# Weight sums made by DMA: an earlier start in the input projection, and all four sums for the last up block

## The chip, the cores and the metric

The kernel runs on one core of a Trainium2 chip. A core has TensorE (PE, matmuls), VectorE (DVE), ScalarE (ACT), GpSimd (POOL) and SyncE (SP), each with a program of its own that it works through in order, and 16 DMA engines that all of them can give transfers to. The metric is the device time of one execution in microseconds (us). The kernel before takes 2088.9 us, the median of three runs (2087.66 to 2093.45).

## The reference, cut to what matters

The block has 512 positions of 2048 channels in float32. An input projection of 4096 columns feeds two token mixers; their normalised outputs go through one output projection; then comes a feed-forward part with 12288 up columns:

```python
h = _rmsnorm(x, norm1_g[l])
p = jnp.einsum('bsd,de->bse', h, w_in[l])
...
y = jnp.concatenate([_rmsnorm(y_gm, gm_out_g[l]), _rmsnorm(y_lru, lru_out_g[l])], axis=-1)
x = x + jnp.einsum('bse,ed->bsd', y, w_out[l])
h = _rmsnorm(x, norm2_g[l])
up = jnp.einsum('bsd,df->bsf', h, ffn_w_up[l])
up = _causal_dwconv(up, ffn_conv_w[l], ffn_conv_b[l])
gate, val = jnp.split(up, 2, axis=-1)
x = x + jnp.einsum('bsf,fd->bsd', jax.nn.gelu(gate) * val, ffn_w_down[l])
```

## The kernel before, in words

**Products in three passes.** Every float32 operand is split into a rounded part h and a rest l (`split`: ACT writes h on L125, DVE writes l = value - h on L126), and each product is three matmuls, h·h, h·l and l·h.

**The projections.** `project` (L171) does one block of 512 columns of the input projection: four chunks `kc` of weights, 1 MB each, loaded by SP into `wraw` (two buffers) and split in two halves of 1024 elements a partition into `wh`/`wl` (three buffers each). It is called eight times; the first call also loads and splits the activations, and is the one with `with_row`. What hangs between the chunks (gates, scans of the recurrent mixer) is passed in as `between`. `out_proj` (L518) does the output projection in the same way, two chunks a call, eight calls: first the four calls of half 1, then the four of half 0. In these stages a scheduler orders the instructions of each engine, except where `manual_schedule` keeps an engine in the order in which the code is written.

**The feed-forward part** works with 2x2 blocks and seven products instead of eight (a Strassen-like scheme). A unit is one block of 256x512 weights; `up_block` (L883) takes 8 units, one for each 256 channels, and has 24 calls in 12 pairs (gate columns, then value columns): units 0 to 191. `down_block` takes the gated rows by chunks of 8, 8 and 6 units for each of four column groups: units 192 to 279. A unit is 7 products of 2 x 3 matmuls (L855), 42 in all. Its seven weight operands are three of the four quarters and four sums of quarters. They are brought by a stream of elements (`Weights`, and `Acts` for the row operands) through three steps: `load` puts the quarters in a slot `q` (three slots; four in the down blocks), `sums` forms the sums on DVE (L609 a pair, then L612 and L613 one each; for `Acts` L636 to L638), `pair` splits all seven (L125 on ACT, L126 on DVE, 1792 elements a partition). `prepare` writes these steps so that the sums of an element stand ahead of the pair of the element before it, on DVE in that order, and a load stands behind the pair that frees its slot.

**Made units.** For some units the sums are not formed on DVE but in memory: POOL issues DMAs that copy a row list of `w_m` into a DRAM tile `made` and then add others to it (`accum_op`), six DMAs for a unit whose four sums are made ("whole"), two for a unit with two sums made ("halved"). SP then loads the made tile (512 KB, or 256 KB for a halved one) and three quarters (384 KB) in place of four quarters (512 KB). A whole unit has no sums on DVE, a halved one keeps L612 and L613. Before the change units 0 to 7, 192 to 199, 216 to 231 and 248 to 261 are whole, and 184 to 191, the last up block, are halved: 46 x 6 + 8 x 2 = 292 DMAs. The 48 of units 0 to 7 stand behind the x loads of the output projection's first half on POOL; the other 244 are handed out by `make` after each unit of the up blocks, evenly over units 0 to 183.

**Who shares POOL's queue.** POOL also issues the loads of gate weights (`graw`, L346), of `vgb`, `ws`, `bsb` and x, and in the up blocks the stores of gated rows (`ad`, L924), four in a row of some 20 us for each pair of blocks, which wait for DVE. In program order the made DMAs of a pair of blocks stand between and behind these four, so they go out in a burst behind the fourth.

**The end of an up block.** `combine` (L868) adds the seven PSUM tiles: ACT copies the first (`c`, L871), DVE does seven additions (L872 to L879), which give the tiles back to PE for the next block. There are 8 such tiles, and a block uses 7. In the order of ACT the copy stands behind the splits that the last unit's `prepare` has written.

Of the kernel before, what the change touches and what calls it, by code (L numbers as in the profile page):

```python
# [8 lines left out]
F32 = mybir.dt.float32  # L9
# [3 lines left out]
ALU = mybir.AluOpType  # L13

P = 128
# [49 lines left out]


def made_units():

    n_up = 24 * 8
    starts = [n_up + 4 * (c[0] - CHUNKS[0][0]) for c in CHUNKS]  # L70
    whole = list(range(8))
    for c, s in zip(CHUNKS, starts):
        whole += range(max(s - 8, n_up), s + len(c))
    return whole, list(range(n_up - 8, n_up))
# [3 lines left out]
def hybrid_block(ctx: ExitStack, tc: tile.TileContext, x, xT, w_in, w_out, w_up, w_dn, w_m4, w_m2, w_dl, wab, wsT, vec, bs, vgb, fg, out):  # L78
# [92 lines left out]
    def project(w, block, act, channel_major, between=None, with_row=None):  # L171
# [7 lines left out]
        for kc in range(4):  # L179
# [12 lines left out]
            if between is not None:  # L192
                between(kc)
        return ps
# [92 lines left out]
    with tc.manual_schedule(engines={E.SP, E.Activation, E.DVE}):  # L287
        px0 = project(w_in, B_X, xg, True, norm1, load_rows)

# [228 lines left out]
    def out_proj(d, half, ysrc, rstd, x_in, between=None):  # L518
        ps = [bank() for _ in range(NS)]
        for c in range(2):  # L520
# [6 lines left out]
            if between is not None:  # L527
                between(c)
        for st in range(NS):
# [26 lines left out]

    in_order = ExitStack()
    in_order.enter_context(tc.manual_schedule(engines={E.Pool}))
# [33 lines left out]
    class Weights:  # L592
# [5 lines left out]
        def load(self):  # L598
# [3 lines left out]
            else:  # L602
                nc.sync.dma_start(q[:, 4 - self.made.shape[1]:4], self.made)
                nc.sync.dma_start(q[:, 4:7], self.src[:, 0:3])

        def sums(self):
            q = self.q
            if self.made is None:
                nc.vector.tensor_tensor(q[:, 2:4], q[:, 5:7], q[:, 7:8].broadcast_to([P, 2, 256]), ALU.add)  # L609
            elif self.made.shape[1] == 4:  # L610
                return
            nc.vector.tensor_tensor(q[:, 1], q[:, 2], q[:, 6], ALU.add)  # L612
# [78 lines left out]
    made = {}  # L691
# [4 lines left out]

    whole, halved = made_units()
    rows = {}  # L700
    for k, u in enumerate(whole):
        t = tc.dram_tile([P, 4, 256], F32, name=f"made{u}")
        flat = t.rearrange("(a b) c d -> a (b c d)", b=2)
        first, second = (w_m4[k, i:i + 512].rearrange("(a b) c -> a (b c)", b=8) for i in (0, 512))
        made[u], rows[u] = t, [[(flat[h], src[h]) for h in (slice(0, 32), slice(32, 64))] for src in (first, second)] + [
            [(t[:, 0:2], w_m4[k, 1024:1280].rearrange("(p a) c -> p a c", p=P))],
            [(t[:, 0], w_m4[k, 1280:1408])],
        ]
    for k, u in enumerate(halved):
        t = tc.dram_tile([P, 2, 256], F32, name=f"made{u}")  # L710
        view = t.rearrange("(a b) c d -> a (b c d)", b=4)
        made[u], rows[u] = t, [[(view, w_m2[k, i * 256:i * 256 + 256].rearrange("(a b) c -> a (b c)", b=8))] for i in range(2)]
# [10 lines left out]
    def make(todo, n):  # L723

        for _ in range(min(n, len(todo))):
            r, dst, src = todo.pop(0)
            how = {"accum_op": ALU.add} if r else {}
            nc.gpsimd.dma_start(dst, src, max_dma_last_dim=8192, **how)  # L728
# [91 lines left out]
    pools["ps"] = psum("q0", 7)  # L820
# [304 lines left out]
```

## Time and profile before

| what | value |
|---|---|
| median of the runs | 2088.9 us |
| the profiled execution: time, and its span | 2092.59 us, 2090.9 us |
| mean granted TensorE clock | 0.995 |
| PE busy | 2045.2 us, 98% |
| DVE busy | 1738.6 us, 83% |
| POOL busy | 283.2 us, of it made DMAs 209.9 us (292 x 863 ns) |
| DMA: software queue (POOL's), hardware queue (SP's) | 24.3%, 34.4% of 16 engines' span |

The table is of one profiled execution. PE is busy nearly all the time, so a gain has to come out of the few stretches in which it stands still or runs at the lower clock; the rows further down show where these are. A busy PE is not PE at its peak, since matmuls overlap: in a stretch the count of matmuls tells more than the busy time.

### The profile page before, as it was taken

The page shows a single profiled execution, that of the slowest core. Times are in us where ns is not written, and L with a number is a line of the kernel's source. Part 1 is how long each engine was busy: PE and PEld are TensorE (multiplying, and loading weights), DVE is VectorE, ACT ScalarE, POOL GpSimd, SP SyncE. Part 2 cuts the span into 40 slices and gives each one's busy share as a digit, 9 for nine tenths or more (in the row PEclk, how much of TensorE's full clock was granted, in tenths as well). Part 3 has the DMA queues.
Part 4 walks back from the last instruction along what each step waited for, and adds up shares of the span by engine and source line. Part 5 has one row for each costly group of instructions (what it writes and reads, how often), then busy time and mean ns, then how long its engine had stood idle before and what let it go on. Part 6 is the DMA issues. An engine that isn't in the chain of part 4 may idle for free.

```text
span 2090.9 us, 34973 instructions
## 1 busy us (share of the span) xinstructions
PE 2045.2 (98%) x14528; PEld 1923.7 (92%) x14528; DVE 1738.6 (83%) x2199; ACT 906.7 (43%) x887; POOL 283.2 (14%) x434
## 2 busy tenths in 40 slices
PE   9999999999989999999999999999998999999998
PEld 7888888888789999999999999999998999999996
DVE  7598982735379999999998999999999989979986
ACT  6445322423264444444444444444455345445343
POOL 1000000033010312212213122122110000000001
PEclk9999999999999999999999999999999999999999
DMA  8222322479263857657658577576566568658564
GB/s 286 92 81 87 115 101 89 157 218 290 85 182 104 212 158 183 179 158 202 177 153 212 141 188 184 155 199 182 151 188 214 191 200 285 190 188 277 182 227 160
DMA packets 102832, 366.93 MB, mean 175 GB/s; under 512 B 14096, under 2 KB 20624, under 8 KB 89232
## 3 DMA queue, kind: packets, MB, share of 16 engines
q1 hardware_dynamic: 65808, 244.20, 34.4%
q0 software_dynamic: 36288, 119.83, 24.3%
q8 instruction: 113, 1.85, 0.4%
q10 hardware_dynamic: 576, 0.66, 0.1%
q14 instruction: 47, 0.39, 0.1%
HBM read 332.13 MB, written 103.02 MB: 208 GB/s over the span
## 4 chain that ended last, share of the span: by engine, by line
PE 71%; DVE 20%; DMA 5%; issue 2%; ACT 1%; SPq 0%; DVEq 0%; ACTq 0%
PE qs L855 42%; PE ps L161 9%; PE ps L163 9%; PE ps L162 9%; DVE wl L126 8%; DMA q<-w_up 4%; DVE q L609 2%; DVE al L126 1%; DVE q L612 1%; DMA q<-ad 1%; DVE cv L919 1%; DVE gate L919 1%; PE qs L162 1%; PE qs L161 1%; PE qs L163 1%
## 5 line engine op out<-in xcount | busy, mean ns | idle before, releaser
L855 PE MATMUL qs<-ah,wh 128*128 128x256 f32 x2688 | 765.3, 285 | 12.3 <-DVE pad L872 8.6
L855 PE MATMUL qs<-ah,wl 128*128 128x256 f32 x2688 | 762.1, 284 | 2.8 <-DVE wl L126 2.8
L855 PE MATMUL qs<-al,wh 128*128 128x256 f32 x2688 | 761.8, 283 | 2.1 <-DVE al L126 2.1
L125 ACT CAST wh<-q 128x1792 fp32r<-128x1792 f32 (+1 forms) x282 | 476.8, 1691 | 593.1 <-PE qs L855 340.8
L126 DVE TENSOR_TENSOR wl<-q,wh 128x1792 fp32r<-128x1792 f32 (+1 forms) x282 | 567.7, 2013 | 47.8 <-ACT wh L125 47.6
L855 PEld LDWEIGHTS qs<-ah,wh 128*128 128x128 f32 x2688 | 517.0, 192 | 16.7 <-DVE pad L872 10.5
L855 PEld LDWEIGHTS qs<-ah,wl 128*128 128x128 f32 x2688 | 516.9, 192 | 3.6 <-DVE wl L126 3.6
L855 PEld LDWEIGHTS qs<-al,wh 128*128 128x128 f32 x2688 | 517.0, 192 | 2.3 <-DVE al L126 2.3
L855 PE MATMUL qs<-wh,ah 128*128 128x256 f32 x1232 | 350.5, 285 | 8.5 <-ACT c L871 4.0
L855 PE MATMUL qs<-wl,ah 128*128 128x256 f32 x1232 | 350.0, 284 | 0.8 <-DVE wl L126 0.6
L855 PE MATMUL qs<-wh,al 128*128 128x256 f32 x1232 | 349.7, 284 | 0.0
L855 PEld LDWEIGHTS qs<-wh,ah 128*128 128x128 f32 x1232 | 237.6, 193 | 9.8 <-ACT c L871 4.2
L728 POOL DMA_DIRECT2D made<-w_m x292 | 209.9, 863 | 268.6 <-DMA made<-w_m 255.5
L855 PEld LDWEIGHTS qs<-wl,ah 128*128 128x128 f32 x1232 | 237.6, 193 | 1.4 <-DVE wl L126 1.4
L855 PEld LDWEIGHTS qs<-wh,al 128*128 128x128 f32 x1232 | 237.6, 193 | 0.0
L126 DVE TENSOR_TENSOR wl<-wraw,wh 128x1024 fp32r<-128x1024 f32 (+2 forms) x105 | 118.0, 1125 | 143.5 <-ACT wh L125 143.2
L125 ACT CAST wh<-wraw 128x1024 fp32r<-128x1024 f32 (+2 forms) x105 | 102.2, 974 | 262.2 <-PE ps L162 136.2
L609 DVE TENSOR_TENSOR q<-q 128x512 f32<-128x512 f32 x226 | 154.9, 685 | 31.5 <-DMA q<-w_up 29.8
L161 PE MATMUL ps<-xgh,wh 128*128 128x512 f32 x384 | 152.8, 398 | 0.1
L162 PE MATMUL ps<-xgl,wh 128*128 128x512 f32 x384 | 152.3, 397 | 0.0
L163 PE MATMUL ps<-xgh,wl 128*128 128x512 f32 x384 | 150.5, 397 | 0.0
L924 POOL DMA_DIRECT2D ad<-gate x48 | 28.1, 585 | 668.0 <-DVE gate L922 631.9
(241 smaller groups left out, 2471.8 us busy)
## 6 DMA issues: line engine op xcount, KB each, us to landing
q<-w_up SPq DMA_DIRECT2D x176, 512.0 KB, 4.1
made<-w_m POOLq DMA_DIRECT2D x246, 256.0 KB, 6.0
wraw<-w_in SPq DMA_DIRECT2D x28, 1024.0 KB, 4.8
q<-w_dn SPq DMA_DIRECT2D x50, 512.0 KB, 3.8
q<-made SPq DMA_DIRECT2D x46, 512.0 KB, 4.0
wraw<-w_out SPq DMA_DIRECT2D x16, 1024.0 KB, 7.4
q<-w_dn SPq DMA_DIRECT2D x38, 384.0 KB, 4.8
ad<-gate POOLq DMA_DIRECT2D x48, 256.0 KB, 2.7
```

Of the source, the lines that this page charges most:

```text
L125: nc.scalar.copy(h, src)
L126: nc.vector.tensor_tensor(l, src, h.bitcast(F32), ALU.subtract)
L161: nc.tensor.matmul(ps, lhsT=ah, rhs=bh, start=start, stop=False)
L162: nc.tensor.matmul(ps, lhsT=ah, rhs=bl, start=False, stop=False)
L163: nc.tensor.matmul(ps, lhsT=al, rhs=bh, start=False, stop=stop)
L609: nc.vector.tensor_tensor(q[:, 2:4], q[:, 5:7], q[:, 7:8].broadcast_to([P, 2, 256]), ALU.add)
L612: nc.vector.tensor_tensor(q[:, 1], q[:, 2], q[:, 6], ALU.add)
L728: nc.gpsimd.dma_start(dst, src, max_dma_last_dim=8192, **how)
L855: nc.tensor.matmul(q[p][:, t], lhsT=x_, rhs=y_, start=first and t == 0 and n == 0, stop=last and t == 1 and n == 2, skip_group_check=True)
L919: nc.vector.scalar_tensor_tensor(dst, pads[n][:, j, i:i + S], col(V_FW + i * 96 + f), dst, ALU.mult, ALU.add)
L924: nc.gpsimd.dma_start(ad[2 * g + n][:, at:at + 2], gate.rearrange("p (a b) -> p a b", a=2))
```

## The change

Three things:

- The eight units of the last up block (184 to 191) become whole: 54 whole units, 324 made DMAs, no list `w_m2`, and no DVE sums for those units. Their loads grow from 256 + 384 KB to 512 + 384 KB.
- Making begins in the input projection. All made DMAs stand in one list, in which the six DMAs of a unit are spread over four steps (its copies, then its additions one step later each, beside those of the units before it). After each chunk of `project` but for the first call POOL gets 4 of them, after each chunk of `out_proj` 2, together 7 x 4 x 4 + 16 x 2 = 144. Ahead of each such group POOL copies one column of the chunk's first `wl` into a tile `pace`, so that the group waits for that split.
- The remaining 180 are handed out over units 0 to 175 of the up blocks. POOL is kept in program order from behind the first projection on, where it was so only from the output projection on.

```diff
+MIX_STEP, OUT_STEP = 4, 2
...
     for c, s in zip(CHUNKS, starts):
-        whole += range(max(s - 8, n_up), s + len(c))
-    return whole, list(range(n_up - 8, n_up))
+        whole += range(s - 8, s + len(c))
+    return whole
...
             if between is not None:
                 between(kc)
+            if with_row is None:
+                make(MIX_STEP, parts[0][1][:, 0, 0:1].bitcast(F32))
...
+    for k, u in enumerate(made_units()):
+        made[u] = t = tc.dram_tile([P, 4, 256], F32, name=f"made{u}")
+        both = t.rearrange("(a b) c d -> a (b c d)", b=2)
+        first, second = (w_m4[k, i:i + 512].rearrange("(a b) c -> a (b c)", b=8) for i in (0, 512))
+        halves_of = (slice(0, 32), slice(32, 64))
+        copies.append([(0, both[h], first[h]) for h in halves_of])
+        added.append(([(1, both[h], second[h]) for h in halves_of], [
+            (1, t[:, 0:2], w_m4[k, 1024:1280].rearrange("(p a) c -> p a c", p=P)),
+            (1, t[:, 0], w_m4[k, 1280:1408]),
+        ]))
...
+    for k in range(len(made) + 3):
+        for n, part in ((k, 0), (k - 1, 1), (k - 2, 2), (k - 3, 3)):
+            if 0 <= n < len(made):
+                to_make += copies[n] if part == 0 else added[n][0] if part == 1 else [added[n][1][part - 2]]
+    pace = const.tile([P, 1], F32, name="pace")
+
+    def make(n, after=None):
+
+        if after is not None:
+            nc.gpsimd.tensor_copy(pace, after)
+        for _ in range(min(n, len(to_make))):
+            add, dst, src = to_make.pop(0)
+            how = {"accum_op": ALU.add} if add else {}
+            nc.gpsimd.dma_start(dst, src, max_dma_last_dim=8192, **how)
+
+    in_order = ExitStack()
+    in_order.enter_context(tc.manual_schedule(engines={E.Pool}))
...
             if between is not None:
                 between(c)
+            make(OUT_STEP, parts[0][1][:, 0, 0:1].bitcast(F32))
...
-                nc.sync.dma_start(q[:, 4 - self.made.shape[1]:4], self.made)
+                nc.sync.dma_start(q[:, 0:4], self.made)
...
-            if self.made is None:
-                nc.vector.tensor_tensor(q[:, 2:4], q[:, 5:7], q[:, 7:8].broadcast_to([P, 2, 256]), ALU.add)
-            elif self.made.shape[1] == 4:
+            if self.made is not None:
                 return
+            nc.vector.tensor_tensor(q[:, 2:4], q[:, 5:7], q[:, 7:8].broadcast_to([P, 2, 256]), ALU.add)
             nc.vector.tensor_tensor(q[:, 1], q[:, 2], q[:, 6], ALU.add)
             nc.vector.tensor_tensor(q[:, 0], q[:, 1], q[:, 4], ALU.add)
...
-    def in_turn(us):
-
-        todo = []
-        for a, b in zip(us + [None], [None] + us):
-            for u, r in ((a, 0), (b, 2), (a, 1), (b, 3)):
-                if u is not None and r < len(rows[u]):
-                    todo += [(r, dst, src) for dst, src in rows[u][r]]
-        return todo
...
-    order = sorted(rows)
-    to_make = in_turn(order[8:])
-    n_make = len(to_make)
-    make(start_make := in_turn(order[:8]), len(start_make))
-    in_order.close()
...
-            make(to_make, len(to_make) - n_make + n_make * (u0 + m + 1) // (n_up - 8))
+            make(len(to_make) - n_make + n_make * (u0 + m + 1) // (n_up - 16))
```

What this moves on the engines, at three places. The first is POOL in the input projection and the output projection. `graw`, `vgb`, `ws`, `bsb` and x are loads from DRAM, `made` are the DRAM tiles. Before:

```order
L346 DMA graw<-wab 128x256 x3
L477 DMA vgb<-vgb 128x512 x4
L508 DMA ws<-wsT 128x1024
L511 DMA bsb<-bs 128x1024
L509 AFFINE_SELECT ws<-ws 128x1024
L534 DMA x_2807<-x 128x4x512
L534 DMA x_3055<-x 128x4x512
L534 DMA x_3181<-x 128x4x512
L534 DMA x_3307<-x 128x4x512
L728 DMA made_3493<-w_m 32x2048 x4
```

And now, behind the first projection:

```order
L361 MEMSET pad 128x3 x4
L384 DMA graw<-wab 128x256
L318 COPY pace<-wl 128x1
L322 DMA made_556<-w_m 32x2048 x2
L322 DMA made_557<-w_m 32x2048 x2
L384 DMA graw<-wab 128x256
L318 COPY pace<-wl 128x1
L322 DMA made_556<-w_m 32x2048 x2
L322 DMA made_558<-w_m 32x2048 x2
```

The making of unit 0 (made_3493 before, made_556 now) moves from behind the x loads to behind the second gate load, and goes on in groups of four. Before the change the first 10 made DMAs of the up blocks stood at the very start of POOL's program; now one does.

The second place is POOL in a pair of up blocks, from the fourth store of gated rows to the first of the next pair. Before:

```order
L924 DMA ad_3466<-gate 128x512
L728 DMA made_3510<-w_m 32x2048 x2
L728 DMA made_3509<-w_m 128x256
L728 DMA made_3511<-w_m 32x2048 x2
L728 DMA made_3510<-w_m 128x512
L728 DMA made_3511<-w_m 32x2048 x2
L728 DMA made_3510<-w_m 128x256
L728 DMA made_3512<-w_m 32x2048 x2
L728 DMA made_3511<-w_m 128x512
L728 DMA made_3512<-w_m 32x2048 x2
L728 DMA made_3511<-w_m 128x256
L728 DMA made_3513<-w_m 32x2048
```

And now:

```order
L921 DMA ad_3685<-gate 128x512
L322 DMA made_589<-w_m 32x2048 x2
L322 DMA made_588<-w_m 128x512
L322 DMA made_587<-w_m 128x256
L322 DMA made_591<-w_m 32x2048 x2
L322 DMA made_590<-w_m 32x2048 x2
L322 DMA made_589<-w_m 128x512
L322 DMA made_588<-w_m 128x256
L322 DMA made_592<-w_m 32x2048 x2
```

The burst has 12 made DMAs where it had 16, and an addition now stands five or more DMAs behind the one that it builds on, where it stood two or three behind it.

The third place is DVE at the end of the last up block, up to the additions of `combine`. Before:

```order
L612 TENSOR_TENSOR q<-q 128x256
L613 TENSOR_TENSOR q<-q 128x256
L126 TENSOR_TENSOR wl<-q,wh 128x1792
L919 SCALAR_TENSOR_TENSOR cv<-pad_4819,vc,cv 128x512 x2
L922 TENSOR_TENSOR gate<-gate,cv 128x512
L612 TENSOR_TENSOR q<-q 128x256
L613 TENSOR_TENSOR q<-q 128x256
L126 TENSOR_TENSOR wl<-q,wh 128x1792
L612 TENSOR_TENSOR q<-q 128x256
L613 TENSOR_TENSOR q<-q 128x256
L126 TENSOR_TENSOR wl<-q,wh 128x1792
```

And now:

```order
L127 TENSOR_TENSOR wl<-q,wh 128x1792
L916 SCALAR_TENSOR_TENSOR cv<-pad_4958,vc,cv 128x512 x2
L919 TENSOR_TENSOR gate<-gate,cv 128x512
L127 TENSOR_TENSOR wl<-q,wh 128x1792 x2
```

Two additions a unit are gone; the rest stands in the same order. The order of PE is the same in both kernels.

## Rows read from the trace of the kernel before

**Rows 1.** The page's busy times by engine, and its chain of work that ended last, by line.

```profile
PE 2045.2 (98%) x14528; PEld 1923.7 (92%) x14528; DVE 1738.6 (83%) x2199; ACT 906.7 (43%) x887; POOL 283.2 (14%) x434
...
PE qs L855 42%; PE ps L161 9%; PE ps L163 9%; PE ps L162 9%; DVE wl L126 8%; DMA q<-w_up 4%; DVE q L609 2%; DVE al L126 1%; DVE q L612 1%; DMA q<-ad 1%; DVE cv L919 1%; DVE gate L919 1%; PE qs L162 1%; PE qs L161 1%; PE qs L163 1%
```

**Rows 2.** Busy time of each engine by stage: from and to in us, length, PE busy (matmuls), PEld, DVE, ACT, POOL busy (instructions), granted clock, DMA share, GB/s. The stages are the input projection, the two halves of the output projection, the end of the first up block, the other up blocks, the last up block, the change to the down blocks, the first down block, and the rest of them.

```profile
40.00:380.00 340.00, 340.00 (x1460) 273.53 (x1460) 237.93 (x303) 127.04 (x165) 5.55 (x14) 1.00 0.30 99
380.00:475.00 95.00, 95.00 (x458) 79.53 (x457) 56.14 (x90) 29.33 (x38) 23.12 (x32) 1.00 0.68 197
475.00:560.00 85.00, 85.00 (x377) 70.38 (x376) 31.88 (x31) 27.06 (x41) 17.08 (x24) 1.00 0.69 208
...
636.00:1541.00 905.00, 894.02 (x7390) 889.69 (x7391) 848.48 (x1074) 402.13 (x330) 185.10 (x264) 1.00 0.65 174
1541.00:1582.00 41.00, 38.90 (x316) 37.91 (x315) 38.71 (x44) 23.53 (x19) 0.81 (x1) 1.00 0.53 175
1582.00:1596.00 14.00, 8.83 (x51) 8.57 (x52) 13.47 (x17) 6.17 (x6) 0.00 (x0) 0.76 0.46 168
1596.00:1636.00 40.00, 38.23 (x314) 37.63 (x313) 37.70 (x42) 20.53 (x17) 3.31 (x6) 1.00 0.73 246
```

**Rows 3.** The chain of work from 640 to 760 us: start, length, what. The first row is PE alone, without a wait.

```profile
639.88 88.45 PE qs L855 x737
```

**Rows 4.** Who waited for whom from 636 to 1541 us: in total, times, longest.

```profile
DVE q L609 <- DMA q<-w_up: 29.8, 23, 4.4
...
DVE q L612 <- DMA q<-w_up: 1.7, 1, 1.7
```

**Rows 5.** DMA queues (packets, MB, share of 16 engines) and loads (times, KB each, median us to landing) from 736 to 766 us, where no made DMA runs.

```profile
q1 hardware_dynamic: 930, 3.42, 37.8%
...
q<-w_up SPq DMA_DIRECT2D x6, 512.0 KB, 3.5
```

**Rows 6.** The same from 704 to 738 us, in a burst of made DMAs.

```profile
q0 software_dynamic: 1455, 4.29, 62.5%
...
q<-w_up SPq DMA_DIRECT2D x6, 512.0 KB, 6.1
```

**Rows 7.** The chain of work from 1541 to 1600 us, in order of time.

```profile
1546.20 3.24 DMA q<-w_up
...
1564.57 3.30 DMA q<-w_up
...
1577.65 4.40 DMA q<-ad
```

**Rows 8.** Who waited for whom from 1541 to 1596 us, for PE.

```profile
PE qs L855 <- ACT c L871: 4.0, 1, 4.0
...
PE qs L855 <- DVE wl L126: 1.7, 2, 1.2
```

**Rows 9.** ACT in order of time around the end of the last up block.

```profile
1583.72 1.68 ACT L125 CAST ah<-q 128x1792 fp32r<-128x1792 f32 x1 [1.42 <-DVE q L638]
1585.31 0.58 ACT L871 COPY c<-qs 128x512 f32<-128x512 f32 x1
```

**Rows 10.** Busy times and granted clock from 1586 to 1593 us, columns as in rows 2.

```profile
1586.00:1593.00 7.00, 5.77 (x28) 5.51 (x29) 6.65 (x10) 1.48 (x1) 0.00 (x0) 0.55 0.54 206
```

**Rows 11.** Groups of DVE instructions from 1541 to 1595 us: line, form, times, busy and mean ns of one, idle time before.

```profile
L613 DVE TENSOR_TENSOR q<-q 128x256 f32<-128x256 f32 x5 | 2.1, 425 | 0.2
L612 DVE TENSOR_TENSOR q<-q 128x256 f32<-128x256 f32 x5 | 2.1, 423 | 0.6 <-DMA q<-w_up 0.6
```

**Rows 12.** Loads from 1540 to 1640 us: times, KB each, median us to landing.

```profile
q<-made SPq DMA_DIRECT2D x8, 512.0 KB, 3.6
...
q<-w_dn SPq DMA_DIRECT2D x8, 384.0 KB, 4.5
...
q<-w_up SPq DMA_DIRECT2D x4, 384.0 KB, 3.3
q<-made SPq DMA_DIRECT2D x4, 256.0 KB, 2.6
```

**Rows 13.** POOL's made DMAs from 636 to 1541 us: times, busy and mean ns of one, idle time before them and what ended it.

```profile
L728 POOL DMA_DIRECT2D made<-w_m x220 | 159.8, 876 | 146.0 <-DMA made<-w_m 133.3 <-issue 12.5
```

**Rows 14.** POOL in order of time in the pair of blocks around 716 us, behind the fourth store of gated rows: start, length, what, in brackets the idle time before it and what ended it.

```profile
706.63 3.57 POOL L728 DMA_DIRECT2D made<-w_m  x5
...
730.36 1.34 POOL L728 DMA_DIRECT2D made<-w_m  x2 [1.09 <-DMA made<-w_m]
```

**Rows 15.** Weight loads of the input projection from 40 to 380 us, and under them made DMAs and weight loads of the output projection from 440 to 520 us, with queue q0's share there: times, KB each, median us to landing.

```profile
wraw<-w_in SPq DMA_DIRECT2D x27, 1024.0 KB, 4.8
...
q0 software_dynamic: 3366, 10.54, 60.5%
...
made<-w_m POOLq DMA_DIRECT2D x31, 256.0 KB, 6.8
wraw<-w_out SPq DMA_DIRECT2D x7, 1024.0 KB, 8.4
```

**Rows 16.** The chain of work from 560 to 640 us, around the end of the first up block, and under it who waited for whom from 600 to 636 us, for PE.

```profile
609.48 7.85 DMA q<-w_up
...
PE qs L855 <- DVE al L126: 2.1, 1, 2.1
```

More of the change, by code (lines that the diff above doesn't have):

```diff
@@ L64, with hybrid_block @@
 EVAC = 150
+MIX_STEP, OUT_STEP = 4, 2
 def made_units():
-    n_up = 24 * 8
-    starts = [n_up + 4 * (c[0] - CHUNKS[0][0]) for c in CHUNKS]
+    starts = [24 * 8 + 4 * (c[0] - CHUNKS[0][0]) for c in CHUNKS]
     whole = list(range(8))
     for c, s in zip(CHUNKS, starts):
-        whole += range(max(s - 8, n_up), s + len(c))
-    return whole, list(range(n_up - 8, n_up))
+        whole += range(s - 8, s + len(c))
+    return whole
 @with_exitstack
-def hybrid_block(ctx: ExitStack, tc: tile.TileContext, x, xT, w_in, w_out, w_up, w_dn, w_m4, w_m2, w_dl, wab, wsT, vec, bs, vgb, fg, out):
+def hybrid_block(ctx: ExitStack, tc: tile.TileContext, x, xT, w_in, w_out, w_up, w_dn, w_m4, w_dl, wab, wsT, vec, bs, vgb, fg, out):
     nc = tc.nc
@@ L288, in hybrid_block @@
         px0 = project(w_in, B_X, xg, True, norm1, load_rows)
+    made = {}
+    copies, added = [], []
+    for k, u in enumerate(made_units()):
[8 more added lines that the diff above has]
+        ]))
+    to_make = []
+    for k in range(len(made) + 3):
[12 more added lines that the diff above has]
+    in_order.enter_context(tc.manual_schedule(engines={E.Pool}))
     def small(name):
@@ L554, in lru_norm @@
         spatial(c)
-    in_order = ExitStack()
-    in_order.enter_context(tc.manual_schedule(engines={E.Pool}))
     x2[0] = load_x(0)
@@ L690, in hybrid_block @@
     starts = []
-    made = {}
     for c in CHUNKS:
@@ L695, in hybrid_block @@
     n_up = starts[0]
[L699 to L712, printed above, removed]
-    def in_turn(us):
-        todo = []
-        for a, b in zip(us + [None], [None] + us):
-            for u, r in ((a, 0), (b, 2), (a, 1), (b, 3)):
-                if u is not None and r < len(rows[u]):
-                    todo += [(r, dst, src) for dst, src in rows[u][r]]
-        return todo
[L723 to L728, printed above, removed]
-    order = sorted(rows)
-    to_make = in_turn(order[8:])
-    n_make = len(to_make)
-    make(start_make := in_turn(order[:8]), len(start_make))
-    in_order.close()
     def act_tiles(m, shape):
@@ L820, in hybrid_block @@
     pools["ps"] = psum("q0", 7)
+    n_make = len(to_make)
+    in_order.close()
     ctx.enter_context(tc.manual_schedule())
@@ L1085 @@
     units += [w_dn[n, p] for ch in CHUNKS for n in range(4) for p in ch]
-    whole, halved = made_units()
+    whole = made_units()
     def made(us, lists):
@@ L1108 @@
         "w_m4": made(whole, [(0, 2, 1, 2), (3, 3, 3, 3), (1, 1), (2,)]),
-        "w_m2": made(halved, [(1, 2), (3, 3)]),
         "w_dl": c(i["ffn_w_down"][0][TAIL * 2 * P:].reshape(4, P, 4, 512).transpose(2, 1, 0, 3)).reshape(4, P, 2048),
```

## The prediction

> **What bounds the kernel now.** I read the page's busy times and its chain first [rows 1]: PE is busy for 98% of the span and most of the chain is PE's matmuls, so only what PE loses can be gained. The busy times by stage tell where that is [rows 2]. In the input projection and both halves of the output projection PE never stands still (340.0 of 340, 95.0 of 95, 85.0 of 85 us), although DMAs of the software queue fill the engines in the last two. The losses lie further on. A stretch in which PE waits for nothing has 737 matmuls in 88.45 us [rows 3], 0.120 us each; by that the 7390 matmuls from 636 to 1541 us need 886.8 us and took 905, a loss of 18.2 us. The 316 + 51 matmuls from 1541 to 1596 us need 44.0 us and took 55, a loss of 11.0 us in a twentieth of the time. The 314 of the first down block cost 2.3 us more than they need.
>
> Next comes what PE waits for there. In the up blocks DVE is busy 848.5 of 905 us, and of the 56.5 us that are left it stands 29.8 + 1.7 = 31.5 us for the landing of weight loads [rows 2, 4]. That is what PE's 18.2 us come from: DVE has hardly any reserve, and where it has to wait for a load, PE waits later, at a block's end. A load lands in 3.5 us in a quiet stretch and in 6.1 us in a burst of made DMAs, which hold 62.5% of the DMA engines [rows 5, 6]. In the last up block the chain runs through DVE's sums and splits and through loads of 3.24, 3.30 and 4.40 us [rows 7], and ends in one stall of PE: 4.0 us for ACT's copy `c` [rows 8], which stands behind the split of an `Acts` element, and that behind its sums on DVE and its load, issued late because the slot came free late [rows 7, 9]. Behind that stall the granted clock was 0.55 for 7 us [rows 10], so PE ran most of that time at 1.2 GHz and not 2.4.
>
> **The change part by part**, against the profiled execution's span of 2090.9 us.
>
> *Last up block, whole units.* DVE loses 8 x 2 additions of 0.425 and 0.423 us [rows 11]: 6.8 us, all on the chain, since DVE is busy 38.7 of 41 us there [rows 2]. The copy `c` started at 1585.3 us; 6.8 us earlier is 1578.5, before PE has done its last unit (its stall began at about 1581.9, 4.0 us ahead of the copy's end). So the 4.0 us go, and with them the 3.2 us of the low clock (7 x 0.45) and most of the 1.7 us of waits for `wl` [rows 8]. What is late next is DVE's own additions of `combine`, about level with PE. Against this stand the loads: 512 + 384 KB for 256 + 384 KB. The nearest rows are those of the whole units of the same stretch, 3.6 and 4.5 us, beside 2.6 and 3.3 us for halved ones [rows 12], 1.2 us more for the one that lands last. Two legs of the chain are such loads [rows 7], so at worst 2.4 us of the 6.8 come back. Bounds: -11.0 (all that the stretch loses) and -4.4. I take -9.0, near the first, because the stall is one event that needs only 4 us of lead, and its clock loss goes with it.
>
> *Fewer made DMAs in the up blocks.* 220 made DMAs run there now [rows 13]; with 180 handed out, of which the first 8 and some 10 more stand so far ahead on POOL that they go out in the first block, some 162 remain, 26% fewer. The burst behind each pair's fourth store shrinks from 16 to 12 DMAs; it now lasts from 706.6 to 730.4 us and beyond [rows 14]. If DVE's waits shrink with the number, 31.5 x 0.26 = 8.2 us go. PE's loss was 18.2 for 31.5 us of waits, 0.58, so PE gets 4.7 us. Against this: an addition now stands five DMAs or more behind its base, so POOL, which waited 133.3 us for its own DMAs [rows 13], waits less, and more DMAs are in flight at once. The burst gets denser as it gets shorter. The nearest row for dense traffic has the same 60% share for the software queue and lets a 1 MB load land in 8.4 us instead of 4.8 [rows 15], which is no worse than 6.1 against 3.5. Bounds: -13 (each wait gone that a shorter burst can spare, 0.58 x 23), and +6 (the two waits that DVE has in a pair of blocks each 0.5 us longer: 11 x 2 x 0.5 x 0.58). I take -4.7.
>
> A rule of the Trainium skill bears on this (DMA: Bandwidth & Descriptors, Queues, rings and completion order): each DMA engine serves its queues in turn, a packet from each. By it the depth of POOL's queue would not matter to a load, only whether the queue is empty, and the up blocks would give the -4.7 or more; if loads instead had to wait for all that is queued ahead, they would give something near the +6. The trace shows 6.1 us for a load in a burst, and no run here shows a deeper queue.
>
> *First up block.* Its last made load landed in 7.85 us, on the chain, and PE waited 2.1 us behind it [rows 16]. In POOL's program 13 made DMAs stood there; now 10 do, which nothing holds but their own order. I take -1.0, between -2.1 (landing as in the quiet stretch) and +1.0 (the same contention, met one unit earlier).
>
> *Projections.* 112 + 32 made DMAs come in, at most 1.6 us of all 16 engines each, since 31 of them, with some smaller ones and stores, took 60.5% of 80 us [rows 15]. In the input projection the engines are 30% busy [rows 2] and a chunk lasts some 18 us (340 us for some 18.5 chunks), so four of them make it at most 65%. Two raw buffers let a load be late by most of a chunk, and the output projection takes 8.4 us loads without a loss [rows 2, 15]: 0. A cover that could go: `pace` is a new reader of `wl`, so DVE may write that buffer only after POOL has come by. On POOL stand ahead of it the gate loads, `vgb`, x and, in half 0, the stores of x2, which wait for DVE; behind a late copy DVE would stand, and behind DVE PE. A buffer is written again three halves later, two halves or some 18 us of PE's work, and POOL's groups of four take 3.5 us (4 x 0.88 [rows 13]) and more where one waits, so I give it +2 at most. The 10 made DMAs that leave the kernel's start are given nothing, since the page's chain names no load of `w_in` [rows 1].
>
> *Down blocks.* The same order, the same loads. DVE and PE both reach them earlier. 0, within 2 us either way.
>
> Sum: -9.0 - 4.7 - 1.0 = -14.7 us, a span of 2076.2. The median of the runs lies 3.7 us under the profiled execution's 2092.59, so the median goes from 2088.9 to 2074.2 us.
>
> **The rivals.** (1) *Loads take DVE's place in the last up block.* With three slots and larger loads, the block goes at the pace of landings, and only 4.4 us come of it. The three load legs in the chain speak for it [rows 7]; against it, DVE was idle only 2.3 us in that block [rows 2]. Sum -10.1, 2079 us. (2) *Denser bursts eat the gain in the up blocks:* fewer waits, each longer, net nothing. For it, landings nearly double as soon as the software queue is busy [rows 5, 6]; against it, the engines are nearly full in a burst already, so a denser one cannot slow a load much. -10.0, 2079 us; with (1) -5.4, 2083.5. (3) *Slower: dense bursts make both waits of each pair longer.* Loads in a burst would land so late that DVE, which has some 25 us in 905 besides these waits, falls back in every pair: with 1.4 us more on each of 22 waits, 22 x 1.4 x 0.58 = +17.9, less 9.0 is +8.9, 2098 us. It decides from a landing of 6.1 + 0.7 = 6.8 us in bursts (22 x 0.7 x 0.58 = 9.0), and from about 7.3 us the kernel is slower by more than 0.3%. The longest wait of 4.4 us [rows 4] shows that single loads get that late. (4) *The change doesn't do what it says:* the copy `c` is held by something else, such as the load of the rows, which was still 4.40 us [rows 7]: then the stall moves and stays, -2 there and -4 in all, 2085 us.
>
> **How the numbers follow.** 0.3% (6.3 us, about what a measurement of this kernel can tell from no change) lies at 2082.6 us. The forecast has 0.54 (2063 to 2080); (1) 0.13, (2) 0.11, both together 0.06, (3) 0.08, (4) 0.08. Faster by more: the forecast, and most of (1) and (2), 0.77. Within: (4), (1) with (2), and the rest of them, 0.15. Slower: (3), 0.08. The range reaches from all terms at their better bounds short of the last two us, 2063, to 2087, which holds all but (3) and the ends of (4).
>
> **What would show it.** In the profile after: PE's wait for `c` (4.0 us) gone and the clock at 1.00 around the end of the last up block, with some 46 us for the 367 matmuls that took 55; DVE's waits for `q<-w_up` down from 31.5 to some 23 us; loads in bursts at 6 to 7 us; PE busy throughout until the output projection ends. I am wrong if landings in bursts pass 6.8 us, if PE shows gaps before 560 us with DVE's `wl` held by POOL's copy, or if a wait for a load of rows stands where `c` stood.

## The result, and the profile after

The changed kernel takes 2076.1 us (median of 4 runs, 2073.1 to 2078.9); the kernel before, on the same chip, 2091.2 us (4 runs). The ratio is 0.9925, 95% interval 0.9909 to 0.9941: faster, by 15.1 us in the medians, where 14.7 us were forecast. The profiled execution took 2073.06 us with a span of 2071.3 us, 19.6 us less than the span before; that is one execution beside one, and the medians stand for the kernels. The parts of that sum came out otherwise than forecast. Here and below a stretch of the feed-forward part is measured between the starts of product matmuls in the trace, 42 to a unit:

| stretch | before | after | measured | forecast |
|---|---|---|---|---|
| up to the first product of the up blocks | 577.0 | 574.0 | -3.0 | 0 |
| first up block (8 units) | 52.7 | 52.1 | -0.6 | -1.0 |
| the next 22 up blocks (176 units) | 908.0 | 897.4 | -10.6 | -4.7 |
| last up block and first 8 units of the down blocks | 91.8 | 87.4 | -4.4 | -9.0 |
| rest | 461.4 | 460.4 | -1.0 | 0 |

How far two executions of the same code lie apart shows in e8 below, whose feed-forward part is as before: 51.3, 907.7, 90.1 and 459.4 us for the last four rows. So a difference of up to 2 us between single stretches says nothing.

The page after, rows that answer to [rows 1, 13]: busy times, the chain by line, and the group of made DMAs (busy, mean ns, idle time before them and what ended it).

```profile
PE 2037.6 (98%) x14528; PEld 1921.8 (93%) x14528; DVE 1732.0 (84%) x2183; ACT 906.6 (44%) x887; POOL 323.7 (16%) x510
...
L322 POOL DMA_DIRECT2D made<-w_m x324 | 234.9, 1061 | 54.0 <-DMA made<-w_m 44.8
```

PE issues the same 14528 matmuls in 7.6 us less busy time, and POOL waits 44.8 us for its own DMAs where it waited 133.3 in the up blocks alone. By stage (columns as in [rows 2]):

```profile
40.00:380.00 340.00, 340.00 (x1470) 275.30 (x1470) 238.94 (x304) 128.63 (x167) 96.55 (x156) 1.00 0.69 179
380.00:475.00 95.00, 95.00 (x460) 79.98 (x460) 55.94 (x89) 27.70 (x35) 20.50 (x35) 1.00 0.65 192
475.00:560.00 85.00, 84.84 (x377) 70.12 (x376) 32.90 (x32) 28.25 (x47) 19.19 (x30) 1.00 0.63 182
...
636.00:1541.00 905.00, 900.66 (x7480) 898.12 (x7479) 857.97 (x1079) 410.86 (x337) 143.97 (x206) 1.00 0.58 163
```

The reader is to look at the counts. In the up blocks 7480 matmuls fit where 7390 did, 90 x 0.120 = 10.8 us. In the input projection PE is full in both kernels, and yet 1470 fit where 1460 did: each takes less time, which no step of the forecast foresaw. DVE's wait for loads in the up blocks [rows 4], and queues and loads from 700 to 734 us [rows 6], which hold a burst of made DMAs and the quiet behind it:

```profile
DVE q L646 <- DMA q<-w_up: 18.6, 19, 2.5
```

```profile
q0 software_dynamic: 1129, 3.30, 43.9%
...
q<-w_up SPq DMA_DIRECT2D x7, 512.0 KB, 4.3
```

The waits fell from 31.5 to 18.6 us. The 4.3 us is to be read with care: it is a median over loads in the burst and loads behind it. POOL's burst, the loads issued in it (702 to 716 us), those behind it (717 to 734 us), and under them the first two loads of the burst before the change (704 to 716 us):

```profile
702.90 7.86 POOL L322 DMA_DIRECT2D made<-w_m  x11
```

```profile
q0 software_dynamic: 737, 2.11, 67.3%
...
q<-w_up SPq DMA_DIRECT2D x2, 512.0 KB, 8.6
```

```profile
q<-w_up SPq DMA_DIRECT2D x4, 512.0 KB, 3.5
```

```profile
q<-w_up SPq DMA_DIRECT2D x2, 512.0 KB, 7.3
```

So a load in the burst lands later than before, and fewer loads meet a burst. Of the loads of `q<-w_up` that start from 636 to 1541 us, 35 of 178 take over 5 us, where it was 58 of 175; over 8 us take 15, where it was 5.

Last, the end of the last up block: the chain of work (start, length, what), ACT in order of time, and the granted clock behind it [rows 7, 9, 10].

```profile
1558.14 1.95 DVE al L127
1560.10 4.08 DMA q<-ad
1564.21 0.70 DVE q L671
```

```profile
1565.85 1.69 ACT L126 CAST ah<-q 128x1792 fp32r<-128x1792 f32 x1 [1.44 <-DVE q L673]
1567.44 0.58 ACT L868 COPY c<-qs 128x512 f32<-128x512 f32 x1
```

```profile
1567.00:1574.00 7.00, 5.31 (x23) 5.02 (x24) 6.69 (x9) 2.61 (x3) 0.00 (x0) 0.51 0.60 212
```

The stall that was to go is still there. The copy `c` stands behind the cast of an `Acts` element, that behind its sums, those behind a load of rows of 4.08 us, and that load was issued only when DVE's split at 1558.14 gave the slot back. The copy starts 43.9 us behind the last up block's first product, 47.6 before: it came 3.7 us earlier, and PE reaches the next unit 2.6 us earlier. PE waits 3.4 us (4.0 before), and the granted clock behind it is 0.51 of full, the lower of its two levels for nearly all of 7 us.

### The profile page after: what moved, and what is told of

It is laid out like the page before. It is cut to its first block, busy times and chain, and to the rows that moved or that the text cites. A ratio compares the mean times of both kernels' runs of the same rounds, so it can differ in the third digit from the quotient of the medians.

```text
span 2071.3 us, 35056 instructions
## 1 busy us (share of the span) xinstructions
PE 2037.6 (98%) x14528; PEld 1921.8 (93%) x14528; DVE 1732.0 (84%) x2183; ACT 906.6 (44%) x887; POOL 323.7 (16%) x510
## 4 chain that ended last, share of the span: by engine, by line
PE 76%; DVE 17%; DMA 4%; issue 2%; ACT 1%; DVEq 0%; SPq 0%; ACTq 0%
PE qs L852 46%; PE ps L162 9%; PE ps L164 9%; PE ps L163 9%; DVE wl L127 7%; DMA q<-w_up 3%; DVE q L646 2%; DVE al L127 1%; DVE q L647 1%; DVE cv L916 1%; DMA q<-w_dn 1%; PE qs L163 1%; PE qs L162 1%; PE qs L164 1%; DVE gate L916 1%
## 5 line engine op out<-in xcount | busy, mean ns | idle before, releaser
L322 POOL DMA_DIRECT2D made<-w_m x324 | 234.9, 1061 | 54.0 <-DMA made<-w_m 44.8
L646 DVE TENSOR_TENSOR q<-q 128x512 f32<-128x512 f32 x226 | 154.8, 685 | 22.1 <-DMA q<-w_up 18.6
```

## The experiments

All times are compared with the kernel before on the same chip. "Made" counts the made DMAs from 636 to 1541 us, "wait" is DVE's wait there for `q<-w_up` in us, and the matmuls are those of the two windows; 905 us hold 7540 matmuls of 0.120 us.

| kernel | made | wait | matmuls 636-1541 | matmuls 40-380 | median us | ratio, 95% |
|---|---|---|---|---|---|---|
| before | 220 | 31.5 | 7390 | 1460 | | 1 |
| changed | 162 | 18.6 | 7480 | 1470 | 2076.1 | 0.9925 (0.9909-0.9941) |
| e1 | 244 | 38.6 | 7290 | 1461 | 2101.8 | 1.0045 (1.0029-1.0061) |
| e2 | 133 | 9.6 | 7520 | 1471 | 2073.8 | 0.9908 (0.9885-0.9932) |
| e3 | 162 | 12.2 | 7504 | 1472 | 2070.9 | 0.9894 (0.9870-0.9918) |
| e4 | 248 | 55.9 | 7129 | 1472 | 2121.4 | 1.0145 (1.0117-1.0174) |
| e5 | 162 | 18.0 | 7477 | 1471 | 2082.0 | 0.9951 (0.9931-0.9970) |
| e6 | 119 | 0.6 | 7493 | 1316 | 2115.9 | 1.0119 (1.0093-1.0146) |
| e7 | 133 | 11.6 | 7517 | 1471 | 2070.8 | 0.9900 (0.9876-0.9924) |
| e8 | 221 | 29.6 | 7394 | 1469 | 2091.4 | 0.9992 (0.9971-1.0014) |
| e9 | 171 | 2.0 | 7538 | 1472 | 2065.2 | 0.9879 (0.9860-0.9899) |
| e10 | 233 | 3.7 | 7531 | 1461 | 2075.0 | 0.9924 (0.9904-0.9944) |
| e11 | 133 | 9.9 | 7530 | 1471 | 2069.0 | 0.9899 (0.9878-0.9920) |
| e12 | 162 | 21.4 | 7453 | 1472 | 2077.2 | 0.9935 (0.9919-0.9952) |

### The parts of the change alone: e1 to e4

The theory (B in the expectations) was that what counts is how many made DMAs run beside the up blocks; the rivals were the new order of the list (C) and the whole last block (A).

**e1**: the kernel before with only the last up block whole.

```diff
-        whole += range(max(s - 8, n_up), s + len(c))
-    return whole, list(range(n_up - 8, n_up))
+        whole += range(s - 8, s + len(c))
+    return whole, []
```

> The kernel before with one part of the change alone: the last up block's eight units are whole, so that the 48 made DMAs of units 0 to 7 stand where they stood, and 276 instead of 244 are handed out over the up blocks in the old order. If the gain of the last block comes from its missing DVE sums and is bounded by its loads (theory A), that block and the first down block lose some 4.4 us less, and if the up blocks' time goes with the number of made DMAs in them (theory B), DVE's waits for w_up grow from 31.5 to some 35 us and PE loses 2 us more there: about -2 us in all, ratio 0.999. If the order of the additions is what slows the up blocks (theory C), the number matters little: -4 us, ratio 0.998.

**e2**: the changed kernel with the last up block halved as before.

```diff
-        whole += range(s - 8, s + len(c))
-    return whole
+        whole += range(max(s - 8, 24 * 8), s + len(c))
+    return whole, list(range(24 * 8 - 8, 24 * 8))
```

> The changed kernel with the last up block halved as before: 292 made DMAs, 144 of them in the projections, 148 in the up blocks, in the new order. Theory B: waits in the up blocks fall further than in the changed kernel, -11 to -12 us there, -3 us ahead of the up blocks, and the last block loses its 11 us as before: -14 us, ratio 0.993. If the whole block were what the gain hangs on (theory A alone), it would be near -3 us, ratio 0.9985.

**e3**: the changed kernel with the list in the order of before.

```diff
-    for k in range(len(made) + 3):
-        for n, part in ((k, 0), (k - 1, 1), (k - 2, 2), (k - 3, 3)):
+    for k in range(len(made) + 1):
+        for n, part in ((k, 0), (k - 1, 2), (k, 1), (k - 1, 3)):
```

> The changed kernel with its list in the order of before (a unit's additions two or three DMAs behind their base), paced the same. Theory B (the number of made DMAs in the up blocks decides): as the changed kernel, -15 us, ratio 0.9925, with POOL's waits for its own DMAs back at some 100 us. Theory C (the order of the additions decides, since POOL waits less and its bursts are shorter): the up blocks lose most of their 10.7 us again, -6 us, ratio 0.997.

**e4**: the changed kernel without made DMAs in the input projection.

```diff
-MIX_STEP, OUT_STEP = 4, 2
+MIX_STEP, OUT_STEP = 0, 3
```

> The changed kernel without made DMAs in the input projection: 48 in the output projection (3 after each chunk, paced), 276 in the up blocks, in the new order. Theory B: the up blocks have more made DMAs than before the change, so their 10.7 us are lost and some 2 us more, the last block's 4.4 us stay: -2 to -3 us, ratio 0.999. Theory C: the up blocks keep most of their gain: -12 us, ratio 0.994. The 2.6 us that the input projection gained go if they come from the DMAs that run beside it, and stay if they come from where tiles lie.

The early start is the gain: e2 and e3 keep it and are as fast as the changed kernel or faster, and so is e7 further down, which has neither the whole last block nor the new order; e1 and e4 lack it and are slower than before. The whole last block alone makes the kernel slower: 24 more made DMAs run in the window, and 100 matmuls fewer fit, 12 us (e1). Beside the early start it is worth nothing that can be measured (e2): the last up block and the 8 units behind it take 87.4 us whole and 90.1 halved, but the 176 units ahead of them 897.4 and 893.5, so that the 29 more made DMAs seem to take back what the block gives. The new order isn't the gain either (e3). With many made DMAs left to the up blocks, the new order goes with a far larger loss, which nobody had expected: e4, with 4 more than e1, loses another 161 matmuls, 19 us. Bursts of e1 (713 to 747 us), then of e4 (709 to 743 us), then POOL in e4:

```profile
q0 software_dynamic: 1464, 4.23, 65.1%
...
q<-w_up SPq DMA_DIRECT2D x6, 512.0 KB, 6.5
```

```profile
q0 software_dynamic: 1891, 5.32, 74.2%
...
q<-w_up SPq DMA_DIRECT2D x6, 512.0 KB, 8.0
```

```profile
713.38 0.59 POOL L921 DMA_DIRECT2D ad<-gate  x1 [3.70 <-DVE gate L919]
713.95 7.92 POOL L322 DMA_DIRECT2D made<-w_m  x11
```

Eleven made DMAs go out in 7.92 us, none of which waits for its base, and a load of 512 KB takes 8.0 us in that burst. The number alone doesn't decide, then: e4 has 4 more than e1. The pace at which a burst begins doesn't either: the changed kernel sends eleven in 7.86 us, as fast as e4, but one more and it is done at 715 us, where e4 goes on to 734 us. What might count is how many are in flight together, and for how long.

### Density or number: e9, e10

To tell density and number apart, **e9** is e3 with a small ACT copy behind each unit's products, on which POOL waits ahead of the unit's made DMA. They go out one a unit instead of behind the last store.

```diff
+            tick = bn[:, (u0 + m) % 4, (u0 + m) // 4 % 2, 0:1]
+            nc.scalar.copy(tick, col(0))
-            make(len(to_make) - n_make + n_make * (u0 + m + 1) // (n_up - 16))
+            make(len(to_make) - n_make + n_make * (u0 + m + 1) // (n_up - 16), tick)
```

> The changed kernel with the list in its old order (e3: the same 162 made DMAs beside the up blocks) and a small ACT copy behind each unit's products, which POOL reads ahead of the unit's made DMA, so that they go out one a unit, 5 us apart, and not in a burst behind each pair's last store. If the density of the bursts is what costs: a load in the worst stretch of a pair lands in some 4 us instead of 5.3, DVE's waits for q<-w_up fall from 12.2 to below 5 us, and PE does the 176 units from the second up block to the last but one in 889 to 892 us instead of 895.6: 2066 us, ratio 0.987. If only their number counts: waits of 10 to 14 us and 0.989 to 0.990. Rival: the ACT copies or POOL's waits delay the stores of ad or the splits, slower than e3 by 3 us or more, ratio above 0.991.

**e10** is the kernel before with the same pacing and nothing else.

```diff
+            tick = bn[:, (u0 + m) % 4, (u0 + m) // 4 % 2, 0:1]
+            nc.scalar.copy(tick, col(0))
+            nc.gpsimd.tensor_copy(pace, tick)
             make(to_make, len(to_make) - n_make + n_make * (u0 + m + 1) // (n_up - 8))
```

> The kernel before (220 made DMAs beside the up blocks, last up block halved) with nothing but the same pacing in the up blocks. If the density of the bursts is what costs: DVE's waits for q<-w_up fall from 31.5 to below 12 us, the 176 units from 908 to some 897 us, ratio 0.994 to 0.996. If only the number counts: waits of 28 to 34 us, ratio 0.999 to 1.001. A middle result would say that both count.

Spread out, the number costs next to nothing. e10 has no early start, and 233 made DMAs in the window where before had 220; it gains as much as the whole change. DVE's waits (both rows as in [rows 4]), the up blocks by stage, queues and loads from 700 to 734 us, and some of POOL's rows in order of time:

```profile
DVE q L609 <- DMA q<-w_up: 2.2, 4, 1.2
DVE q L612 <- DMA q<-w_up: 1.5, 3, 0.6
```

```profile
636.00:1541.00 905.00, 905.00 (x7531) 904.91 (x7531) 864.86 (x1096) 425.17 (x516) 272.78 (x455) 1.00 0.70 181
```

```profile
q0 software_dynamic: 880, 2.75, 34.8%
...
q<-w_up SPq DMA_DIRECT2D x7, 512.0 KB, 3.8
```

```profile
723.53 0.50 POOL L895 COPY vvar<-bn 128x1 f32<-128x1 f32 x1 [4.12 <-ACT bn L894]
723.98 0.51 POOL L728 DMA_DIRECT2D made<-w_m  x1
727.93 0.41 POOL L895 COPY vvar<-bn 128x1 f32<-128x1 f32 x1 [3.44 <-ACT bn L894]
728.43 0.85 POOL L728 DMA_DIRECT2D made<-w_m  x1
```

The DMA engines are even busier than before over the stage (0.70 against 0.65) and the loads' waits are nearly gone, 3.7 of 31.5 us: an average share says nothing of this cost. e9, with both means, has the lowest ratio of all, 0.9879, though its interval overlaps with e3's, and 7538 of 7540 matmuls in that window: there is hardly more to gain there. Its up blocks by stage:

```profile
636.00:1541.00 905.00, 904.69 (x7538) 904.39 (x7538) 862.36 (x1084) 429.03 (x519) 227.69 (x394) 1.00 0.64 168
```

### More of them early: e6, e7, e11

**e6** is e3 with six made DMAs instead of four after each chunk of the input projection.

```diff
-MIX_STEP, OUT_STEP = 4, 2
+MIX_STEP, OUT_STEP = 6, 2
```

> The changed kernel with the list in its old order (e3) and six made DMAs instead of four at each step of the input projection: 168 + 32 early, 124 left for the up blocks. Theory B (what counts is how many run beside the up blocks): DVE's waits for q<-w_up from 12.2 us (162 DMAs there) to some 7 us (some 106), PE's busy time from 636 to 1541 us from 902.3 to some 904 of 905, 2 to 3 us less than e3: 2068 us, ratio 0.988. Rival: the projections pay, since the DMA share there goes from 0.71 to some 0.9: PE shows gaps before 475 us, with DVE's writes of wl held by POOL's copy, 3 us or more, ratio 0.991 or above.

The waits in the up blocks went to 0.6 us, and the kernel became 45 us slower than e3: the rival, at fifteen times the size that was put on it. The stages of e6, then who waited there (40 to 475 us), then queues and loads from 120 to 200 us in e6 and in e3:

```profile
40.00:380.00 340.00, 315.54 (x1316) 248.53 (x1316) 224.41 (x290) 118.03 (x152) 125.90 (x190) 0.98 0.77 191
380.00:475.00 95.00, 87.72 (x400) 71.56 (x399) 49.57 (x74) 29.30 (x39) 29.31 (x42) 0.96 0.72 196
```

```profile
ACT wh L126 <- DMA wraw<-w_in: 58.5, 11, 11.1
...
PE ps L163 <- DVE wl L127: 14.4, 13, 2.7
```

```profile
q0 software_dynamic: 2623, 7.99, 51.2%
...
wraw<-w_in SPq DMA_DIRECT2D x6, 1024.0 KB, 8.2
```

```profile
q0 software_dynamic: 2161, 6.56, 43.2%
...
wraw<-w_in SPq DMA_DIRECT2D x7, 1024.0 KB, 6.8
```

Of 1472 matmuls (e3) 156 are missing in the first stage, 36 us at 0.231 us each, and 60 of 460 in the second, 12 us at 0.207. POOL's copy `pace` isn't what holds DVE; no row names it. ACT waits 58.5 us for loads of `w_in`, up to 11.1 us for one; e3 has no such wait there. So the reserve of the projections, two raw buffers, ends between four and six made DMAs a chunk.

**e11** is e3 with `MIX_STEP, OUT_STEP = 4, 4`, more in the output projections instead; **e7** is e3 with the last block halved (the edit of e2).

> The changed kernel with the list in its old order (e3) and four made DMAs instead of two at each step of the output projections, so that some 130 instead of 162 are left for the up blocks. By the fit of the runs so far (waits for q<-w_up of 12 us at 162 or 133 and of 1 at 119) the 176 units take 890 to 893 us instead of 895.6, and the output projections, whose loads of w_out landed in 8.4 us in the kernel before without a loss, lose nothing: 2067 us, ratio 0.988. Rival, from six at each step of the input projection: loads of w_out come too late, PE shows gaps between 380 and 560 us of 5 us or more, ratio above 0.991.

> Early start and the list in its old order, with the last up block halved as in the kernel before: some 133 made DMAs in the up blocks instead of 162. Theory B: DVE's waits for q<-w_up from 12.2 to some 8 us, and 2 us less in the up blocks; if the whole block is worth the 4.4 us that it showed, that is lost again: 2071 to 2073 us, ratio 0.990 to 0.991. If the whole last block is worth nothing, as the changed kernel beside e2 says, 2068 us, ratio 0.988 to 0.989.

Neither can be told from e3 (0.9899 and 0.9900 beside 0.9894). In e11 PE stays full in the output projections (460 and 375 matmuls) and the up blocks gain 26 matmuls on e3, 3 us, which is at the limit of what the runs can show.

### The input projection: e8

**e8** is the kernel before with the tile `pace` alone, in the place at which the change allocates it.

```diff
+    pace = const.tile([P, 1], F32, name="pace")
+    nc.gpsimd.memset(pace, 0.0)
```

> The kernel before with nothing but the tile pace (4 bytes a partition, set once on POOL) in the place at which the change allocates it. If the 2.6 us that the input projection lost come from where the tiles behind it lie in SBUF: 1470 matmuls from 40 to 380 us instead of 1460, and ratio 0.9985. If they come from the DMAs or from POOL's order by hand: 1460 matmuls, ratio 1.000. (Without the DMAs beside it, e4 had 1472, which speaks for the place.)

Its stage from 40 to 380 us:

```profile
40.00:380.00 340.00, 339.64 (x1469) 274.55 (x1469) 239.22 (x306) 129.25 (x169) 5.59 (x14) 1.00 0.30 102
```

1469 matmuls instead of 1460, with the same instructions in the same order on PE and no DMA added: 9 x 0.23 = 2 of the 3.0 us come with this tile, not with anything that the change is about. Besides the tile only one memset on POOL is new, so the likely cause is where the tiles behind it lie; no run shows that by itself. All kernels with that tile there have 1469 to 1472, those without it (before, e1, e10) 1460 or 1461; e6, which stalls, is left aside.

### The last up block: e5, e12

**e5** is the changed kernel with the next `prepare` held back in the last unit, so that `c` is ahead of the cast on ACT.

```diff
-            prepare(ready(u0 + m))
+            prepare(ready(u0 + m) if u0 + m < n_up - 1 else place[u0 + 9])
```

> The changed kernel, with the preparation of the next unit behind the last up block's last unit held back to the place of the second row element, so that the copy c stands ahead of the split of the Acts element on ACT. Theory A (c waits only because the split ahead of it waits for the load of the rows): PE's wait for c of 3.4 us falls below 1 us, the granted clock stays at 1.00 there, and 3 to 6 us go: 2070 to 2073 us, ratio 0.990 to 0.991. Rival: the Acts element that comes later is then what PE waits for, in the first pair of the down block, 0 to 4 us, and the ratio stays at 0.9925 or rises to 0.994.

The stall for `c` and its low clock are gone, and no more than the runs can show is won: the last up block and the 8 units behind it take 86.8 us, 87.4 in the changed kernel, and the whole run isn't faster. PE's waits in e5 from 1565 to 1612 us, and the busy times there:

```profile
PE qs L852 <- DVE wl L127: 2.6, 2, 2.3
PE qs L852 <- DVE pad L869: 1.6, 1, 1.6
```

```profile
1565.30:1611.70 46.40, 41.79 (x338) 40.61 (x337) 43.76 (x48) 22.56 (x16) 3.23 (x6) 1.00 0.60 205
```

PE now waits for DVE's splits, and DVE is busy 43.8 of 46.4 us. That read as if DVE's own work were the bound. **e12** leaves out 8 of its instructions there, 6.0 us: the tap additions of the last up block, so that this part of the convolution is missing from its result.

```diff
-            for i in (1, 0):
+            for i in (1, 0) if u0 < n_up - 8 else ():
```

> The kernel of e5 (copy c ahead of the split of the Acts element) with the eight scalar_tensor_tensor of the last up block's taps left out, 8 x 0.749 = 6.0 us of DVE in the first down block; this part of the computation is missing, so only its time is read. In e5 the stall for c was gone and DVE worked nearly without a break in the first 47 us of the down blocks, while PE's wait turned up at DVE's wl. If DVE's own work is what bounds these 47 us: the 336 matmuls of the first four units pairs' stretch (46.4 us in e5, 47.1 in the changed kernel, 40.3 at full pace) take 41 to 43 us, and the kernel takes 3 to 6 us less than the changed one. If loads of rows or the order on ACT bound them: 46 us still, and no change of the total.

That theory fell. The 8 units take 46.5 us as before, with DVE busy 39.9 us. PE's clock hides a little of it: granted 0.96 here and 1.00 in e5, which is 46.5 x 0.04 = 1.9 us. Without that the stretch would take some 44.6 us, an estimate, still above the 41 to 43 that were expected for this theory. The same stretch of e12, then the chain and DVE in it:

```profile
1571.10:1617.60 46.50, 42.77 (x338) 41.96 (x337) 39.94 (x44) 23.84 (x18) 3.22 (x6) 0.96 0.65 217
```

```profile
1578.59 1.94 DVE al L127
...
1580.55 0.32 SPq L639
...
1580.91 5.29 DMA q<-w_dn
```

```profile
1588.02 2.02 DVE L127 TENSOR_TENSOR wl<-q,wh 128x1792 fp32r<-128x1792 f32 x1 [2.10 <-ACT wh L126]
...
1598.51 0.69 DVE L671 TENSOR_TENSOR q<-q 128x512 f32<-128x512 f32 x1 [1.87 <-DMA q<-ad]
```

What DVE saved it spends waiting for loads, which are issued when its own split gives a slot back: the split at 1578.6 frees the slot, the load of 5.29 us follows, ACT's cast, and DVE's next split at 1588.0. In this stretch the ring of slots and landings sets the pace. That more slots would shorten it wasn't tried.

## Why the prediction came out right, and where its steps did not

**The sum** was right by two errors of opposite sign: -10.6 where it had -4.7, and -4.4 where it had -9.0; the 3.0 of the input projection came from neither. That it came out is luck. The two profiled executions lie 19.6 us apart, the forecast had 14.7 for them; only the medians, 15.1 us apart, agree with it.

**Last up block.** The step that failed is "The copy `c` started at 1585.3 us; 6.8 us earlier is 1578.5 ... So the 4.0 us go". It moved the copy by the whole of the work removed from DVE. But the copy hangs on a load, and the load on a slot that a split gives back; the copy came 3.7 us earlier, not 6.8, and PE 2.6 us earlier to the same place. This is rival (4)'s mechanism, the load of rows (4.40 us before, 4.08 after), with rival (1)'s price of -4.4. (The sum given for rival (4) doesn't follow from its terms: -2 with -4.7 and -1.0 is -7.7, not -4.) e5 and e12 show more: with the stall for `c` removed, and then 6 us of DVE's work too, the stretch still takes as long, but for the 1.9 us that the clock took in e12. A stall is the place where a slow ring shows, not a sum that can be taken out.

**Up blocks.** The direction and the mechanism held: waits for `q<-w_up` fell, and PE got the time. The term was mis-sized. "If DVE's waits shrink with the number" gave 8.2 us; they fell by 12.9, although a load in the burst lands later than before (8.6 us, 7.3 before), because fewer loads meet a burst (35 over 5 us, 58 before). Why by more than the number isn't settled: what all these loads took beyond 3.5 us each fell from 214 to 169 us, 21%, and the waits by 41%, so a wait isn't in proportion to a late landing. And PE got 10.6 of these 12.9, not 0.58 of them; the share isn't a constant (e3 12.4 of 19.3, e10 14.5 of 27.8). e10 shows the cause behind the count: the same number, spread out, costs almost nothing.

**The rivals.** (2) rested on "a denser one cannot slow a load much", and that is wrong: 6.1 us at a share of 62.5%, 6.5 at 65.1% (e1), 8.0 at 74.2% (e4), and 8.6 in the changed kernel's own burst. (3) was put at a landing of 6.8 us for no gain and 7.3 for slower by 0.3%. Loads in the changed kernel's burst passed both, and it is faster: (3) let each pair have two such waits, but only the first loads of a short burst meet it, and DVE waited 19 times, 2.5 us at the longest, where it had waited 24 times, 4.4 at the longest. In e4, where 42 loads took over 6.8 us (22 in the changed kernel), DVE waited 33 times, 6.5 us at the longest, and the kernel is 1.45% slower. So (3)'s mechanism is real, and the smaller number in a burst is what kept the change from its price.

**The rule of the Trainium skill** (DMA: Bandwidth & Descriptors, Queues, rings and completion order) is that each DMA engine serves its queues in turn, a packet from each. The prediction drew from it that a load depends on whether POOL's queue has work, not on how much stands in it, and that the up blocks would give the 4.7 us or more. They gave 10.6, but not for that reason: how much is in flight counts. Of the loads beside which the software queue held 70 to 80% of the engines, the 20 of the kernel before, with 3.3 made DMAs in flight, took 6.4 us (medians), and the 11 of the changed kernel, with 6.9 in flight, 8.7 us. Which mechanism does this no run shows; nor do these rows show in what order an engine took its packets.

**First up block.** -0.6 of -1.0, within its bounds; but e8, with nothing changed there, is 1.4 us below the kernel before, so nothing can be read from it. **Projections.** No PE gap came, as forecast. The DMA share rose to 0.69, above the "at most 65%": a chunk doesn't last 18 us. 27 loads in 340 us [rows 15] are one every 12.6 us, so four made DMAs of 1.6 us come to 0.51 beside the 0.30, not 0.35. The cover that was named as able to go, `pace` ahead of DVE's writes, never did; what lies next to the edge is the landing of `w_in` (e6), which the forecast had thought covered by "most of a chunk". **The stated tests** came out so: waits at 18.6 us where 23 were expected; landings in a burst at 8.6 us where 6 to 7 were, so that the sign of being wrong that was set at 6.8 us came, while the kernel got faster: it asked how late a load lands, and not how many do; PE full until the output projection ends; and the two on the last up block, the stall and the clock, did not come.

## What to carry to other kernels

Look at when background transfers go out, not only at how many there are: here a store that waits on its engine's queue dammed up the transfers behind it, and one small wait per step spread them and was worth as much as moving 144 of 324 elsewhere. Read a landing in the burst itself: a median over a window that also holds quiet came out at half of it. Before moving transfers under a stage that looks free, ask how late its own loads may land; four a chunk cost nothing and six cost 48 us. Where a stall hangs on a load that hangs on a slot, don't book the stall as gain when work ahead of it is removed.

## What the runs showed of the hardware

- The median time of a 512 KB load over a stretch of 34 us rose with the share of the software queue in it: 3.8 us at 34.8% (e10), 4.3 at 43.9% (changed), 6.1 at 62.5% (before), 6.5 at 65.1% (e1), 8.0 at 74.2% (e4).
- A single load took the longer the more made DMAs were in flight beside it, on the mean of its first 3.5 us: 3.6 us with less than half a one (123 loads), 4.3 with about one (21), both in the changed kernel, 6.4 with about three (31, before), 8.7 with 6.5 to 9 (18, changed).
- One tile of 4 bytes a partition, allocated ahead of others, let 1469 matmuls instead of 1460 run in 340 us of a full PE (0.2315 against 0.2329 us each). Why is open.
- PE ran at the lower level of its clock for some 7 us behind the stall for `c` (granted clock 0.51 from 1567 to 1574 us); with that stall gone (e5) the clock stayed at 1.00 in the same stretch.
